# Projection weights of the second mixer, split into rounded part and remainder by casting and adding transfers instead of by ScalarE and VectorE

## The chip, the cores and the metric

The kernel runs on one core of a Trainium2 chip. Its time is the device time of one execution in microseconds, taken as the median of several runs. TensorE does the matrix products, VectorE and ScalarE the elementwise work, GpSimd (POOL in the profile) a few small operations and the issue of some transfers, SyncE (SP) the issue of most transfers. Sixteen DMA engines move the bytes.

## The reference, cut to what matters

The program is two layers of a hybrid backbone over 512 latent tokens and 256 context tokens of width 1024. The change concerns the mixer of the second layer, a bidirectional gated recurrence with 8 heads of width 128. For every head three column blocks of one input projection are needed, each a 1024 x 128 slice of the weights:

```python
h = jnp.concatenate([h_ctx, h_lat], axis=1)
fq, f_fwd, f_bwd, fi, fog = _split(h @ w_in, ODD_SIZES)      # w_in: (1024, 5 * 1024)
q = _heads(jax.nn.silu(fq), HGRN_HEADS)
for d, f in enumerate((f_fwd, f_bwd)):
    log_f = jnp.logaddexp(jnp.log(lb[d]), jnp.log1p(-lb[d]) + jax.nn.log_sigmoid(_heads(f, HGRN_HEADS)))
    k = -jnp.expm1(log_f)
    dirs.append(_directional_scan(q, k, i, log_f, n_ctx, reverse=(d == 1)))
o_lat = _gated_readout(dirs[0][1] + dirs[1][1], og[:, :, n_ctx:], out_norm)
```

All values are 32-bit floats.

## The kernel before, in words

**Three products for one.** A product of two 32-bit matrices is made of three products in the faster `float32r` type: each operand is split into a rounded part H and a remainder L = x - H, and H·H + H·L + L·H is accumulated (`mm3`, `gemm_T`). The activations are split beforehand. The weights are split as they arrive, in `fetched`/`unit` (L793 to L806): SyncE loads a unit of 1024 floats per partition into a `raw` tile (L799), ScalarE writes H by a casting copy (L803), VectorE writes L by a subtraction (L804). H and L lie in tiles with the tags `wH` and `wL`, four buffers each, `raw` has three.

**The stage.** `odd_mixer` runs over the 8 heads. `prep(hd)` makes, for direction 0, then direction 1, then the query, one product of a weight unit with the activations: `ff` twice (768 tokens, in a group of 256 and one of 512) and `fq` once (512 tokens). So the heads use 24 units in the order forward gate, backward gate, query. Between them stands the work of the recurrence of earlier heads: ScalarE copies and VectorE multiplications in turn (`qkh`, L1012; `arr`, L1017), small products (`pch`, `pbh`, `knph`, `pdh`, `kcT`, `poh`, `S`), and `rs`, a power on GpSimd (L686), whose result VectorE needs at once (L1489). Generators are advanced in a written-out order:

```python
for hd in range(8):
    given = []
    new = prep(hd, given)
    go(scan, new)
    go(outs, old)
    go(new, new)
    go(outs, old, scan)
    go(new, new)
    go(scan, scan)
```

**What sets the order.** Inside this loop `self.pinned` is true: every TensorE instruction keeps its place in program order (`pin`). ScalarE, VectorE and GpSimd work that isn't pinned is put in order by the framework's scheduler, which simulates the program with its own costs and issues what is ready; what is pinned stays behind all that the program has issued before it on that engine. On the chip each engine then runs its list strictly in that order, waiting where an operand isn't there yet. A tile gets a buffer of its tag when an earlier tile of that tag is done with.

After the heads, `gate` takes the units of the output gate through `wide_units`, by the same `unit`. The feed-forward block's down projection, earlier in the program, already contains transfers that add to what lies in SBUF: 36 of them, issued by GpSimd with `accum_op=ALU.add` (L1773), in pieces of 2 KB. The units of the second mixer are read from the weights in pieces of 128 floats, 512 bytes.

Of the kernel before, what the change touches and what calls it, by code (L numbers as in the profile page):

```python
# [316 lines left out]
class Net:  # L317
# [472 lines left out]
    def unit(self, src, k, n, pool=None, to=None):  # L790

        return self.fetched(src, k, n)(pool, to)
# [607 lines left out]
    def odd_mixer(self, h, fi):  # L1400
        nc, I = self.nc, self.I
        w = I["odd_w_in"][0]
        with self.pool("hg") as gp:
            ones = gp.tile([P, CTX], F32, tag="ones", name="ones")
            nc.gpsimd.memset(ones, 1.0)
            def prep(hd, given):

                f = gp.tile([P, 2, SEQ], F32, tag="f", bufs=2, name=f"f{hd}")
                arr = gp.tile([P, 4, SEQ], F32, tag="arr", bufs=2, name=f"arr{hd}")
                ks = gp.tile([P, SEQ], F32, tag="ks", bufs=2, name=f"ks{hd}")  # L1410
                S0, kcs = [], []
                for d in range(2):
                    pt = self.mm_tile(f"ff{hd}{d}")
                    W = self.unit_cols(w, (1 + d) * D + hd * P)
                    self.gemm_T(pt, W, h, ((512, 256),))
                    yield
                    self.gemm_T(pt, W, h, ((0, 512),))
                    sg = gp.tile([P, NT], F32, tag="sg", bufs=2, name="sg")
                    nc.scalar.activation(sg, pt[:, :NT], AF.Sigmoid)
                    lb, lb1, nlb1 = (x[:, d, hd : hd + 1] for x in (self.lb, self.lb1, self.nlb1))  # L1420
                    fc = gp.tile([P, CTX + 32], F32, tag="fc", bufs=2, name="fc")
                    kc = gp.tile([P, CTX], F32, tag="kc", bufs=2, name="kc")
                    nc.vector.tensor_scalar(fc[:, :CTX], sg[:, SEQ:], lb1, lb, op0=ALU.mult, op1=ALU.add)
                    nc.scalar.activation(kc, sg[:, SEQ:], AF.Identity, bias=lb1, scale=nlb1)
                    nc.vector.tensor_scalar(f[:, d, :], sg[:, :SEQ], lb1, lb, op0=ALU.mult, op1=ALU.add)
                    nc.scalar.activation(arr[:, 2 * d, :], sg[:, :SEQ], AF.Identity, bias=lb1, scale=nlb1)

                    pr = gp.tile([P, CTX], F32, tag="pr", bufs=1, name="pr")
                    if d == 0:
                        nc.vector.memset(pr[:, CTX - 1 : CTX], 1.0)  # L1430
                        nc.vector.tensor_tensor_scan(
                            pr[:, 0 : CTX - 1][:, ::-1], fc[:, 1:CTX][:, ::-1], ones[:, 1:CTX], 1.0, op0=ALU.mult, op1=ALU.mult
                        )
                    else:
                        nc.vector.memset(pr[:, 0:1], 1.0)
                        nc.vector.tensor_tensor_scan(
                            pr[:, 1:CTX], fc[:, 0 : CTX - 1], ones[:, 1:CTX], 1.0, op0=ALU.mult, op1=ALU.mult
                        )
                    nc.vector.tensor_tensor(kc, kc, pr, op=ALU.mult)

                    kcs.append(kc)
                    yield
                pq = self.mm_tile(f"fq{hd}")
                self.gemm_T(pq, self.unit_cols(w, hd * P), h, ((0, 512),))
                q = gp.tile([P, SEQ], F32, tag="q", bufs=2, name=f"q{hd}")
                nc.scalar.activation(q, pq[:, :SEQ], AF.Sigmoid)
                nc.vector.tensor_tensor(q, q, pq[:, :SEQ], op=ALU.mult)
                nc.vector.tensor_tensor(arr[:, 1, :], q, f[:, 1, :], op=ALU.mult)
                nc.vector.tensor_tensor(arr[:, 3, :], q, f[:, 0, :], op=ALU.mult)
                nc.vector.tensor_tensor(ks, arr[:, 0, :], arr[:, 2, :], op=ALU.add)  # L1450
                given.append((arr, q, ks, f, S0))
                yield
                kns = []
                for kc in kcs:
                    pk = self.tr_tile("kcT")
                    for i in range(2):
                        self.tr(pk[:, i * P : (i + 1) * P], kc[:, i * P : (i + 1) * P], self.ident)
                    kn = gp.tile([P, CTX], F32, tag="kcn", bufs=2, name="kcn")
                    nc.scalar.copy(kn, pk[:, :CTX])
                    kns.append(kn)  # L1460
                yield
                pS = self.sc_tile("S0")
                for d, kn in enumerate(kns):
                    for i in range(2):
                        self.mm(
                            pS[:, d * P : (d + 1) * P],
                            kn[:, i * P : (i + 1) * P],
                            fi[:, LT + i, hd * P : (hd + 1) * P],
                            start=(i == 0),
                            stop=(i == 1),  # L1470
                        )
                for d in range(2):
                    S = gp.tile([P, P], F32, tag="S0", bufs=4, name=f"S0{hd}{d}")
                    nc.scalar.copy(S, pS[:, d * P : (d + 1) * P])
                    S0.append(S)

            def head(hd, arr, q, ks, f, S0):
                def V(t, hh):
                    return fi[:, t, hd * P : (hd + 1) * P]

                def evac(hh, t0, n, po):
                    o = fi[:, 0:LT, hd * P : (hd + 1) * P]
                    nc.scalar.copy(o, po)
                    sq = gp.tile([P, LT, P], F32, tag="sq", bufs=1, name="sq")
                    nc.scalar.activation(sq, po, AF.Square)
                    ss = self.sm.tile([P, LT], F32, tag="ss4", name="ss4")
                    nc.vector.tensor_reduce(ss, sq, axis=AX.X, op=ALU.add)
                    rs = self.rstd(ss, P, LT)
                    nc.vector.tensor_tensor(o, o, rs[:, :, None].to_broadcast([P, LT, P]), op=ALU.mult)  # L1489

                return self.scan(gp, f"h{hd}", arr, q, ks, 1.0, f, LT, 1, V, S0, None, evac)

            def gate(c0, early):
                us = self.wide_units(4 * D + c0)
                for t0 in (0, 2):
                    s = self.wp.tile([P, WU], F32, tag="mraw", bufs=2, name="silu").rearrange("p (a n) -> p a n", a=2)

                    def apply(x, t0=t0, s=s):
                        o = fi[:, t0 + x.start : t0 + x.stop, c0 : c0 + 512]
                        nc.vector.tensor_tensor(o, o, s[:, x, :], op=ALU.mult)  # L1500

                    for a in range(2):
                        pt = self.mm_tile("nat")[:, :512]
                        self.wide_tile(pt, us, h, t0 + a)
                        nc.scalar.activation(s[:, a, :], pt, AF.Silu)
                        if t0 or not early:
                            apply(slice(a, a + 1))
                        yield
                    if early and t0 == 0:
                        apply(slice(0, 2))  # L1510

            def go(*xs):
                for x in xs:
                    next(x, None)

            self.pinned = True
            outs = old = scan = iter(())
# [9 lines that stand above are left out]
                outs, old, scan = scan, new, head(hd, *given[0])  # L1527
            g = [gate(0, False), gate(512, True)]
            go(scan, g[0])
            go(outs, old)  # L1530
            go(g[0])
            go(outs, old, scan)
            go(g[0], g[0])
            go(scan, scan)
            go(g[1])
            go(scan)
            go(g[1])
            go(scan)
            go(g[1], g[1])
            self.pinned = False  # L1540

        cat = Split(h.pool)
        for _ in self.gated_T(lambda t, hh: fi[:, t, hh * P : (hh + 1) * P], 8, R_HG, cat, ((0, 4),)):
            pass
        return cat
# [739 lines left out]
```

## Time and profile before

| | |
|---|---|
| median of 3 runs | 1674.94 us (1674.29 to 1675.55) |
| the profiled execution | 1675.78 us, its span 1674.0 us |
| busy over the span | PE 1644.8, DVE 1311.1, ACT 916.1, POOL 129.4 us |
| granted TensorE clock | 0.998 |
| the 24 units of the heads | used from 982 to 1219 us |
| one head, 1094.97 to 1126.50 us | 31.53 us: PE 31.53, DVE 25.13, ACT 19.69, POOL 1.43 busy |

PE is TensorE's matmuls, PEld its weight loads, DVE is VectorE, ACT ScalarE, POOL GpSimd. In a row of groups stand the line, the engine, the operation, output<-inputs, the number of instructions, the busy time, the mean of one in ns, and the idle time just before them with what ended it. All transfers issued by GpSimd run in the queue q0, those of SyncE in q1.

### The profile page before, as it was taken

Reading aid. Unit: us, or ns where it says so; the run is one execution under the profiler, and the core shown is the slowest. Engines: PE = TensorE matmul, PEld = TensorE weight load, DVE = VectorE, ACT = ScalarE, POOL = GpSimd, SP = SyncE. Lnnn points to the kernel's source line nnn. Section 1 sums busy time; section 2 is a strip of 40 time slices with the busy share of each in tenths; the row PEclk is TensorE's granted clock in tenths of the full one; section 3 lists DMA queues with packets and bytes.
Section 4 is the critical chain, followed back from the end, with each engine's and each line's share of the span. In section 5 each row is a group of like instructions: output and inputs, shape, how many; then the busy total and the mean of one; then the engine's idle time right before and its main releaser. Section 6 shows DMA issues by size and latency. Waiting matters only on the chain.

```text
span 1674.0 us, 32524 instructions
## 1 busy us (share of the span) xinstructions
PE 1644.8 (98%) x13407; PEld 1481.1 (88%) x13407; DVE 1311.1 (78%) x2097; ACT 916.1 (55%) x1551; POOL 129.4 (8%) x139
## 2 busy tenths in 40 slices
PE   9999999999999999999999999999999999999998
PEld 7899987888999999998887888888888899999886
DVE  5999678976898988777668648788775599987887
ACT  5745567845544443446447436666664565555664
POOL 2004110011000000002102000000000100000310
PEclk9999999999999999999999999999999999999999
DMA  9641012164243445249525541121124333333973
GB/s 336 213 132 41 3 45 86 50 227 160 80 126 114 139 151 176 78 153 205 100 84 193 200 127 57 48 65 40 51 65 150 126 114 115 114 101 102 226 164 138
DMA packets 184736, 204.79 MB, mean 122 GB/s; under 512 B 7142, under 2 KB 141836, under 8 KB 184588
## 3 DMA queue, kind: packets, MB, share of 16 engines
q1 hardware_dynamic: 173996, 181.98, 34.7%
q0 software_dynamic: 9024, 17.30, 5.9%
q10 hardware_dynamic: 1568, 3.43, 0.6%
q8 instruction: 105, 1.72, 0.4%
q14 instruction: 43, 0.35, 0.1%
HBM read 193.23 MB, written 9.46 MB: 121 GB/s over the span
## 4 chain that ended last, share of the span: by engine, by line
PE 83%; DVE 8%; ACT 3%; DMA 3%; issue 2%; POOL 0%; SPq 0%; DVEq 0%; ACTq 0%; POOLq 0%
PE nat L355 12%; PE a L355 10%; PE ff L355 8%; PE E L355 7%; PE oproj L355 6%; PE x L355 6%; PE o L355 5%; PE D L355 4%; PE b L355 3%; PE fq L355 3%; PE gqk L355 2%; PE pearly L355 2%; PE q L355 2%; PE S L355 2%; PE poh L355 1%
## 5 line engine op out<-in xcount | busy, mean ns | idle before, releaser
L355 PE MATMUL nat<-wH,x 128*128 128x256 f32 (+2 forms) x968 | 226.7, 322 | 1.2 <-ACT x L2014 0.6
L860 ACT CAST wH<-raw 128x1024 fp32r<-128x1024 f32 x120 | 124.8, 1051 | 102.7 <-DVE raw L885 40.7
L355 PEld LDWEIGHTS nat<-wH,x 128*128 128x128 f32 x968 | 161.9, 190 | 19.5 <-ACT natq L1196 1.7
L861 DVE TENSOR_TENSOR wL<-raw,wH 128x1024 fp32r<-128x1024 f32 x120 | 145.7, 1222 | 23.6 <-ACT wH L860 23.3
L355 PE MATMUL nat<-wL,x 128*128 128x256 f32 (+2 forms) x484 | 153.5, 317 | 1.8 <-DVE wL L804 1.8
L804 DVE TENSOR_TENSOR wL<-raw,wH 128x1024 fp32r<-128x1024 f32 x79 | 95.8, 1222 | 50.6 <-ACT wH L803 49.8
L355 PE MATMUL ff<-x,wH 128*128 128x512 f32 (+1 forms) x512 | 127.6, 340 | 0.0
L686 POOL TENSOR_TENSOR rs<-ms,neghalf 128x1 f32<-128x1 f32 (+2 forms) x56 | 60.1, 1076 | 777.7 <-DVE ms L684 777.6
L803 ACT CAST wH<-raw 128x1024 fp32r<-128x1024 f32 x79 | 82.2, 1050 | 68.5 <-PE ff L355 19.7
L355 PE MATMUL oproj<-wH,x 128*128 128x512 f32 x320 | 102.2, 394 | 0.4 <-ACT x L1330 0.4
L355 PEld LDWEIGHTS nat<-wL,x 128*128 128x128 f32 x484 | 92.1, 190 | 7.8 <-DVE wL L804 2.7
L615 DVE SCALAR_TENSOR_TENSOR macc<-mraw,scT,macc 128x1024 f32<-128x1024 f32 x70 | 88.0, 1282 | 11.6 <-DMA mraw<-in_mod_w_dram 11.4
L355 PEld LDWEIGHTS ff<-x,wH 128*128 128x128 f32 x512 | 87.3, 190 | 10.0
L355 PE MATMUL x<-wH,two 128*128 128x512 f32 x280 | 90.5, 392 | 0.9 <-DVE y L1851 0.7
L1773 POOL DMA_DIRECT2D t<-in_ffn_w_down_dram x36 | 41.9, 1200 | 640.1 <-DVE t L1812 338.3
L1012 ACT COPY qkh<-arr 128x512 f32<-128x512 f32 x112 | 70.2, 641 | 36.6 <-DVE arr L1017 32.3
L355 PE MATMUL ff<-x,wL 128*128 128x256 f32 (+1 forms) x256 | 86.2, 337 | 0.0
L885 DVE TENSOR_TENSOR raw<-raw 128x512 f32<-128x512 f32 x120 | 82.8, 690 | 2.8
L1017 DVE TENSOR_TENSOR arr<-arr,f 128x512 f32<-128x512 f32 x112 | 74.4, 688 | 2.0 <-ACT qkh L1012 0.3
L355 PEld LDWEIGHTS oproj<-wH,x 128*128 128x128 f32 x320 | 59.9, 188 | 13.0 <-ACT x L1330 1.0
L355 PE MATMUL a<-T,wH 128*128 128x384 f32 (+1 forms) x320 | 70.5, 309 | 0.6 <-ACT qb L923 0.5
L355 PE MATMUL E<-T,wH 128*128 128x384 f32 (+1 forms) x320 | 70.4, 309 | 0.7 <-DVE go L938 0.7
(425 smaller groups left out, 4558.6 us busy)
## 6 DMA issues: line engine op xcount, KB each, us to landing
mraw<-in_mod_w_dram SPq DMA_DIRECT2D x80, 512.0 KB, 4.4
raw<-in_ffn_w_gate_dram SPq DMA_DIRECT2D x44, 512.0 KB, 3.9
raw<-in_ffn_w_up_dram SPq DMA_DIRECT2D x44, 512.0 KB, 4.9
raw<-in_odd_w_in_dram SPq DMA_DIRECT2D x40, 512.0 KB, 3.7
t<-in_ffn_w_down_dram POOLq DMA_DIRECT2D x30, 512.0 KB, 8.3
raw<-in_ffn_w_down_dram SPq DMA_DIRECT2D x28, 512.0 KB, 8.0
mraw<-in_mod_w_dram SPq DMA_DIRECT2D x32, 256.0 KB, 6.3
raw<-in_even_w_in_dram SPq DMA_DIRECT2D x16, 512.0 KB, 5.9
```

The lines of the kernel that those rows point to most:

```text
L355: return self.pin(self.nc.tensor.matmul(*a, **k))
L615: nc.vector.scalar_tensor_tensor(a, u, w, a, op0=ALU.mult, op1=ALU.add)
L686: nc.gpsimd.tensor_tensor(rs, ms, self.neghalf.to_broadcast([P, w]), op=ALU.pow)
L803: self.casts = self.casts[-1:] + [nc.scalar.copy(H[:, :m], raw[:, :m])]
L804: vector.tensor_tensor(L[:, :m], raw[:, :m], H[:, :m].bitcast(F32), op=ALU.subtract)
L860: self.nc.scalar.copy(H, f)
L861: self.nc.vector.tensor_tensor(L, f, H.bitcast(F32), op=ALU.subtract)
L885: add = lambda o, x, y: nc.vector.tensor_tensor(o, x, y, op=ALU.add)
L1012: nc.scalar.copy(qkv[:, :, :, half, :], dst)
L1017: nc.vector.tensor_tensor(dst, dst, tb, op=ALU.mult)
L1773: add = lambda o, src: self.pin(nc.gpsimd.dma_start(out=o, in_=src, accum_op=ALU.add))
```

## The change

The heads' units are numbered 0 to 23. Units 0 to 2 are fetched as before. For unit n from 3 on, a call of `unit` three units ahead allocates H and L and lets GpSimd issue two casting transfers of 256 KB each from the weights into H (`rounded`). Two units ahead of its use ScalarE writes -H into L, and GpSimd issues two transfers of 256 KB that add the weights to L (`remainder`), so that L = w - H. The `raw` tile, SyncE's load, the casting copy and the subtraction are gone for these 21 units; the four new transfers of each are pinned.

```diff
+            units = {}
+
+            def rows(n):
+                c0 = (D, 2 * D, 0)[n % 3] + n // 3 * P
+                return w[:, c0 : c0 + P].rearrange("(k p) m -> p k m", p=P)
+
+            def rounded(n):
+                H, L = [self.wp.tile([P, WU], F32R, tag=f"w{x}", bufs=4, name=f"w{x}") for x in "HL"]
+                units[n] = [x.rearrange("p (k m) -> p k m", k=KD) for x in (H, L)]
+                for k in (slice(0, 4), slice(4, 8)):
+                    self.pin(nc.gpsimd.dma_start(out=units[n][0][:, k, :], in_=rows(n)[:, k, :]))
+
+            def remainder(n):
+                H, L = units[n]
+                nc.scalar.mul(L, H.bitcast(F32), -1.0)
+                for k in (slice(0, 4), slice(4, 8)):
+                    self.pin(nc.gpsimd.dma_start(out=L[:, k, :], in_=rows(n)[:, k, :], accum_op=ALU.add))
+
+            def unit(n):
+                if n + 3 < 24:
+                    rounded(n + 3)
+                if 3 <= n + 2 < 24:
+                    remainder(n + 2)
+                return units.pop(n) if n in units else self.unit(rows(n), KD, P)
+
...
-                    W = self.unit_cols(w, (1 + d) * D + hd * P)
+                    W = unit(3 * hd + d)
...
-                self.gemm_T(pq, self.unit_cols(w, hd * P), h, ((0, 512),))
+                self.gemm_T(pq, unit(3 * hd + 2), h, ((0, 512),))
```

## The prediction

> **What bounds the kernel now.** I read the page's first part, then the table by stretches for one head, the waits from 980 to 1240 us (the stage of the change), and the chain that ended last through that head.
>
> ```profile
> span 1674.0 us, 32524 instructions
> PE 1644.8 (98%) x13407; PEld 1481.1 (88%) x13407; DVE 1311.1 (78%) x2097; ACT 916.1 (55%) x1551; POOL 129.4 (8%) x139
> 1094.97:1126.50 31.53, 31.53 (x400) 28.10 (x400) 25.13 (x57) 19.69 (x35) 1.43 (x1) 1.00 0.18 52
> PEld pch L355 <- issue: 2.5, 7, 0.4
> PE gcT L358 <- DVE gc L662: 1.0, 1, 1.0
> 1099.62 8.35 PE ff L355 x48
> 1118.48 5.44 PE fq L355 x24
> 1126.50 2.88 PE ff L355 x24
> 1129.37 1.34 PE pdh L355 x12
> ```
>
> The third row is one head: PE is busy 31.53 of 31.53 us at clock 1.00, DVE 25.13, ACT 19.69, POOL 1.43, the DMA engines 18% of the time. The waits list many pairs, but only two in which TensorE stands (total, times, longest): 1.0 us once, at the start of the stage, for VectorE's `gc`, and 0.4 us a head in its own sequencer. The last four rows are the chain (start, duration): products one behind the other. They hide no wait: the 24 large matmuls inside the 8.35 us of `ff` take 8.35 - 2.88 = 5.47 us, the 24 equal ones of `fq` 5.44. TensorE sets the pace of the stage, and VectorE and ScalarE wait for it or for each other.
>
> **The change, part by part.**
>
> *What goes from VectorE and ScalarE.*
>
> ```profile
> L804 DVE TENSOR_TENSOR wL<-raw,wH 128x1024 fp32r<-128x1024 f32 x27 | 33.0, 1224 | 29.8 <-ACT wH L803 29.6
> L803 ACT CAST wH<-raw 128x1024 fp32r<-128x1024 f32 x26 | 27.3, 1049 | 36.0 <-PE ff L355 19.7 <-PE fq L355 16.1 <-PE nat L355 0.3
> ```
>
> VectorE loses 21 subtractions of 1.224 us, 25.7 us in all or 3.7 a head. ScalarE loses 21 casts and gets 21 negations of the same shape, which I take at the same 1.05 us: nothing. All of this ran beside TensorE, so on the path it saves 0. At most the 1.0 us wait for `gc` shrinks, behind fewer subtractions; I take 0. SyncE loses 21 loads; nobody waited for them in the stage.
>
> *What is added on GpSimd and the DMA queues.* 84 transfers of 256 KB in 512-byte pieces, 12 a head. The nearest rows are the adding transfers of the down projection, in 2 KB pieces, in a stretch (800 to 825 us) where little else moves, and SyncE's present loads of the same weights (1000 to 1200 us):
>
> ```profile
> 802.68 0.91 POOL L1773 DMA_DIRECT2D t<-in_ffn_w_down_dram  x1 [23.77 <-DVE wL L1807]
> 806.94 1.22 POOL L1773 DMA_DIRECT2D t<-in_ffn_w_down_dram  x1 [3.35 <-DVE wL L1807]
> q0 software_dynamic: 1301, 2.50, 65.2%
> q1 hardware_dynamic: 267, 0.51, 6.8%
> t<-in_ffn_w_down_dram POOLq DMA_DIRECT2D x5, 512.0 KB, 5.8
> t<-in_ffn_w_down_dram POOLq DMA_DIRECT2D x1, 256.0 KB, 4.2
> ...
> q1 hardware_dynamic: 17728, 10.49, 18.2%
> 1113.48 1.43 POOL L686 TENSOR_TENSOR rs<-ms,neghalf 128x4 f32<-128x4 f32 x1 [30.09 <-DVE ms L684]
> ```
>
> Issue: 128 pieces (256 KB) cost GpSimd 0.91 us, 256 pieces 1.22. A new transfer has 512; another 256 at 0.31 per 128 make 1.84. Bounds: 0.91 (pieces don't count) and 3.6 (proportional). I take 1.84, along the line through the two rows: 12 x 1.84 + 1.43 = 23.5 of 31.5 us. GpSimd stays under the period.
>
> Bytes: a 2 KB piece that adds took 0.652 x 25 x 16 / 1301 = 0.20 us of an engine, a plain one of about 2 KB 0.068 x 25 x 16 / 267 = 0.102, a plain one of about 0.5 KB 0.182 x 200 x 16 / 17728 = 0.033. Plain cost goes nearly with the bytes (a third at 0.6 KB), so I take a third of 0.20, 0.065 us, for an adding 512-byte piece; bounds 0.033 and 0.20. For a casting one, which no row shows, the same bounds, and 0.033 to 0.065. Each engine gets 32 pieces of a transfer: a head's 192 + 192 pieces take 192 x (0.065 + 0.033 to 0.065) = 19 to 25 us of 31.5. They fit too.
>
> Landing: 256 KB landed in 4.2 = 0.91 + 8 x 0.20 + 1.7, 512 KB in 5.8 = 1.22 + 16 x 0.20 + 1.4. So a transfer lands 1.5 us after its issue, plus its pieces.
>
> *Where the new waits stand.* On GpSimd the first casting transfer of unit n+3 waits for TensorE's last matmul with unit n-1, whose buffer it takes. Behind it are queued its second half, the two adding transfers of unit n+2 (which wait for ScalarE's negation), and the next `rs`. Tightest is the second `ff` unit of a head: `ff` ends at 1118.48; casting transfers issue to 1122.2, adding ones to 1125.8, and the last adding pieces land at about 1130. TensorE wants them at 1105.09 + 31.53 = 1136.6 (1105.09 is where that `ff` began, 1099.62 + 5.47). 6 us are left. `rs` at 1113.48 comes after four issues that start at 1105.1 and end at 1112.5: free.
>
> On ScalarE a negation waits for the landed H, and what is listed behind it waits as well:
>
> ```profile
> 1118.73 1.05 ACT L803 CAST wH<-raw 128x1024 fp32r<-128x1024 f32 x1
> 1121.03 0.80 ACT L1426 ACTIVATE arr<-sg,lb,nlb 128x512 f32<-128x512 f32 x1
> 1124.68 0.59 ACT L1446 ACTIVATE q<-fq 128x512 f32<-128x512 f32 x1
> 1126.22 0.87 ACT L1064 COPY knh<-knph 128x384 f32<-128x384 f32 x2
> ACT wH L803 <- DMA raw<-in_odd_w_in_dram: 3.3, 2, 2.0
> ```
>
> The scheduler orders ScalarE by its own idea of when H lands; the last row (whole run) shows it early by up to 2.0 us. After 1121.8 ScalarE is free until `fq` ends, so the negation for the unit cast from 1118.48 on may be listed ahead of `q`. H's second half lands at 1118.48 + 2 x 1.84 + 1.5 + 32 x 0.033 = 1124.7, with 0.065 us a piece (the first half in the way) at 1126. Then negation, `q`, and 2.41 us from the start of `q` to the end of `knh`. `pdh` needs `knh` at 1129.37: `q` may start at 1126.96, H may land at 1125.9. So it just holds; I take 0, and every microsecond later costs 1 us in each of six heads (the units 8, 11, ... 23). The other two negations of a head have more room: what they hold back is next needed 5 us later or more.
>
> *The start.*
>
> ```profile
> 949.38 1.05 ACT L803 CAST wH<-raw 128x1024 fp32r<-128x1024 f32 x1 [2.01 <-DMA raw<-in_odd_w_in_dram]
> 981.13 1.05 ACT L803 CAST wH<-raw 128x1024 fp32r<-128x1024 f32 x1
> 998.78 1.05 ACT L803 CAST wH<-raw 128x1024 fp32r<-128x1024 f32 x1 [3.78 <-PE ff L355]
> 999.87 1.23 DVE L804 TENSOR_TENSOR wL<-raw,wH 128x1024 fp32r<-128x1024 f32 x1 [4.05 <-ACT wH L803]
> 999.26 0.39 PE L355 MATMUL fq<-x,wL 128*128 128x512 f32 x1
> ```
>
> Before, units 0 to 3 are cast by 981.13 into the four buffers. Now units 3, 4 and 5 are asked for before 0, 1 and 2 respectively, so six units share four buffers, and unit 2, the first query, can end up with the buffer that unit 1 frees at 998.8. Its cast and subtraction then take the place that unit 5's had in the rows: L is there at 999.87 + 1.23 = 1001.10, and the first matmul with L, at 999.26 before, waits 1.8 us. Ends: 0 if unit 2 gets an earlier buffer, 3 if the first adding transfers come late too. I take 1.8, as six units can't lie in four buffers.
>
> *Sum.* Against the profiled execution, 1675.78 us: 0 + 0 + 1.8 = 1677.6. That execution is 0.84 above the median of the three runs, so 1676.8 stands against 1674.94. That is 0.11%; 0.2%, or 3.35 us, is about what a measurement of this kernel can tell from no change.
>
> [...]
>
> **The rivals.**
>
> *ScalarE is held by a landing (slower).* The place is the negation ahead of `q`; it decides from H landing over 7.4 us after `ff` ends. For it: the issue queue of GpSimd stands ahead of the landing, the 2.0 us row, and 7.9 us was the median landing in the busier down projection. Against: VectorE is 3.7 us a head less loaded, and the cast at 1118.73 no longer stands ahead. At 1 to 3 us late: 6 to 18 us, 1683 to 1695, mid 1687.
>
> ```profile
> DMA to landing us min/median/max: 4.2/7.9/12.2
> ```
>
> *The DMA engines become the bound (slower).* If a piece costs 0.20 us whatever its size, when it adds: a head takes 192 x (0.20 + 0.033) = 44.7 us against 31.5, over seven heads 92 us: 1767. Cast pieces at 0.20 as well make 76.8 a head and 1992. It decides from 0.131 us an adding piece. Against: plain pieces get cheaper with size.
>
> *GpSimd becomes the bound (slower).* It decides from 2.5 us an issue (12 x 2.5 + 1.43 = 31.4). At 3.0, 37.4 us a head, 41 us in seven: 1716. Against: the two measured issues lie on a flat line.
>
> *VectorE's relief is worth something (faster).* Its 25.13 of 31.53 us fall to 21.4, and if the 1.0 us and all seven sequencer waits of 0.4 went, 3.5 us: 1671.4. Against: no other wait of TensorE is there to remove.
>
> **How the numbers follow.** Forecast (start only, 1676.8): 0.50. ScalarE held: 0.29, of which 0.03 stay within 0.2%. DMA bound 0.10. GpSimd bound 0.06. Faster 0.05. So slower by over 0.2%: 0.26 + 0.10 + 0.06 = 0.42; within: 0.53; faster: 0.05. The forecast's own range is 1674 to 1678.3. To leave out no more than 2 in 10 it must reach over the held ScalarE: up to 1700, with the two bounds (0.16) and a gain of over 1 us (0.03) outside.
>
> **What would show it.** Right: the period of a head stays 31.5 us with PE full; a DVE of about 21.4 a head; GpSimd's issues near 1.8 us; no wait of PE for ScalarE or DMA after 1010 us; a wait of up to 2 us before the first `fq`. Wrong: PE waiting for `knh` in every head with ScalarE's `wL` waiting for a transfer (first rival), for `wL` itself with q0 busy all the time (second) or with GpSimd busy all the time (third). The weakest step is the price of a 512-byte casting or adding piece, which no row shows.

## The result, and the profile after

The changed kernel takes 1702.43 us (median of 3 runs, 1699.45 to 1705.98) against 1674.94: 1.0165 of the time before, interval 1.0133 to 1.0197. The profiled execution is the slowest of the three, 1705.98 us with a span of 1704.2, so its numbers run some 3.5 us above the median. The forecast was 1676.8 with a range up to 1700: the time lies 25.6 us above the one and 2.4 us outside the other.

The first part and the transfers of the page of after:

```profile
span 1704.2 us, 32616 instructions
PE 1657.3 (97%) x13407; PEld 1490.7 (87%) x13407; DVE 1289.6 (76%) x2076; ACT 913.4 (54%) x1551; POOL 215.1 (13%) x223
wH<-in_odd_w_in_dram POOLq DMA_DIRECT2D x42, 256.0 KB, 3.7
wL<-in_odd_w_in_dram POOLq DMA_DIRECT2D x42, 256.0 KB, 4.7
```

The same number of products now keeps PE busy 12.5 us longer, and the span grows by 30.2. VectorE loses 21.5 us, GpSimd gains 85.7. The table by stretches (length, then PE, PEld, DVE, ACT, POOL busy, clock, DMA share, GB/s), for two heads in the middle of the stage and for the last one, in which only two casting and four adding transfers are left to issue:

```profile
1062.00:1100.30 38.30, 34.22 (x398) 30.39 (x397) 22.07 (x54) 19.25 (x34) 13.68 (x13) 0.91 0.56 84
1100.30:1137.80 37.50, 34.10 (x398) 30.27 (x397) 22.69 (x55) 19.51 (x35) 13.60 (x13) 0.91 0.58 86
1211.90:1243.50 31.60, 31.60 (x400) 28.17 (x399) 26.02 (x62) 21.20 (x37) 8.15 (x7) 1.00 0.47 85
```

A head went from 31.53 to some 38 us. Some 3.4 to 4.1 us of that is PE standing still, and some 2.6 is PE busy for longer, at a mean clock of 0.91. No engine but PE is near full and the DMA engines are little over half busy, so the columns alone name no bound. The waits of the stage (970 to 1290 us; total, times, longest) do:

```profile
POOL wL L1422 <- issue: 83.2, 31, 5.6
ACT wL L1420 <- DMA wH<-in_odd_w_in_dram: 73.1, 16, 9.3
DVE arr L1017 <- ACT qkh L1012: 42.8, 6, 8.9
POOL wH L1416 <- issue: 42.6, 17, 3.9
PE poh L355 <- DVE Sh L1084: 9.7, 5, 2.2
PE poh L355 <- ACT kcn L1484: 4.9, 4, 1.9
PE pdh L355 <- DVE CTh L997: 2.7, 1, 2.7
PE fq L355 <- ACT wH L803: 0.9, 1, 0.9
PE fq L355 <- DVE wL L804: 0.5, 1, 0.5
```

Read from the bottom: TensorE stands 17.3 us in three new waits inside the heads and 1.4 us at the first `fq`. With the 12.5 us of longer busy time that is 31.2, against 30.2 of growth. The first row is the surprise. "Issue" is time in which the engine waited for nothing that the profile shows: GpSimd stood 126 us, 18 a head, ahead of transfers whose operands were there. Its timeline (start, duration, idle before):

```profile
1019.74 1.31 POOL L1422 DMA_DIRECT2D wL<-in_odd_w_in_dram  x1
1024.60 1.30 POOL L1422 DMA_DIRECT2D wL<-in_odd_w_in_dram  x1 [3.55 <-issue]
1025.45 1.23 POOL L1416 DMA_DIRECT2D wH<-in_odd_w_in_dram  x1
1029.67 0.76 POOL L1416 DMA_DIRECT2D wH<-in_odd_w_in_dram  x1 [2.99 <-issue]
```

An issue is cheap, some 0.8 us for a casting transfer and 1.3 for an adding one; but in the four transfers of a unit GpSimd stops twice for about 3 to 4 us, about until something earlier has landed: the add issued at 1019.74 landed 4.5 us later, and the next one starts at 1024.60. The waits on GpSimd in the two heads from 1062 to 1137.8 us:

```profile
POOL wL L1422 <- issue: 26.2, 9, 5.5
POOL wH L1416 <- issue: 12.5, 4, 3.9
POOL wH L1416 <- PE ff L355: 5.0, 2, 2.9
POOL wL L1422 <- ACT kc L1449: 2.1, 1, 2.1
POOL wL L1422 <- ACT arr L1451: 2.1, 1, 2.1
```

Issuing and `rs` 13.68 + 13.60 = 27.3 us, stops 38.7: 33.0 us a head, more than the 31.53 that TensorE needs. The two waits of 2.1 us, put down to ScalarE, look like stops too: each ends 0.3 us after the landing of the first of the two casting transfers ahead of it (issued at 1063.12 and 1101.91, landed 3.4 us later). With them it is 35.1 us a head. The last 5.0 us, for the buffer of `ff`, are the way back: GpSimd waits for a TensorE that is late. The chain shows how GpSimd's load reaches TensorE (start, duration):

```profile
1111.90 0.77 POOL wH L1416
1112.67 3.94 issue
...
1116.62 3.38 DMA wH<-in_odd_w_in_dram
...
1120.07 1.06 ACT wL L1420
1121.13 0.56 ACT qkh L1012
...
1121.71 1.29 DVE arr L1017 x2
...
1127.56 3.35 PE poh L355 x14
```

The second half of an H is issued 3.94 us late, lands at 1120.0, and holds ScalarE's negation; `qkh` is listed behind the negation, VectorE's `arr` (L1017) waits for `qkh`, `Sh` for `arr`, and `poh` for `Sh`. TensorE, late, frees the next buffer late, and the next casting transfer starts late again.

### The profile page after: what moved, and what is told of

The parts are those of the page before. It is cut to its first block, busy times and chain, and to the rows that moved or that the text cites. A ratio compares the mean times of both kernels' runs of the same rounds, so it can differ in the third digit from the quotient of the medians.

```text
span 1704.2 us, 32616 instructions
## 1 busy us (share of the span) xinstructions
PE 1657.3 (97%) x13407; PEld 1490.7 (87%) x13407; DVE 1289.6 (76%) x2076; ACT 913.4 (54%) x1551; POOL 215.1 (13%) x223
## 4 chain that ended last, share of the span: by engine, by line
PE 72%; DVE 10%; issue 7%; ACT 4%; DMA 3%; POOL 3%; DVEq 0%; SPq 0%; POOLq 0%; ACTq 0%
PE nat L355 12%; PE a L355 10%; PE E L355 7%; PE x L355 7%; PE oproj L355 6%; PE o L355 5%; PE b L355 3%; PE D L355 3%; PE ff L355 3%; PE gqk L355 2%; PE pearly L355 2%; POOL wL L1422 2%; PE q L355 2%; PE S L355 1%; PE attO L355 1%
## 5 line engine op out<-in xcount | busy, mean ns | idle before, releaser
L860 ACT CAST wH<-raw 128x1024 fp32r<-128x1024 f32 x120 | 124.8, 1051 | 100.7 <-DVE raw L885 38.7
L861 DVE TENSOR_TENSOR wL<-raw,wH 128x1024 fp32r<-128x1024 f32 x120 | 145.8, 1222 | 24.0 <-ACT wH L860 23.4
L686 POOL TENSOR_TENSOR rs<-ms,neghalf 128x1 f32<-128x1 f32 (+2 forms) x56 | 59.2, 1062 | 561.2 <-DVE ms L684 561.0
L1017 DVE TENSOR_TENSOR arr<-arr,f 128x512 f32<-128x512 f32 x112 | 73.9, 689 | 44.5 <-ACT qkh L1012 42.8
L804 DVE TENSOR_TENSOR wL<-raw,wH 128x1024 fp32r<-128x1024 f32 x58 | 70.1, 1222 | 34.0 <-ACT wH L803 33.2
L1012 ACT COPY qkh<-arr 128x512 f32<-128x512 f32 x112 | 69.0, 637 | 30.2 <-DVE arr L1017 26.1
L803 ACT CAST wH<-raw 128x1024 fp32r<-128x1024 f32 x58 | 60.1, 1050 | 39.1 <-PE nat L355 17.0
L355 PE MATMUL E<-x,wH 128*128 128x384 f32 (+1 forms) x320 | 70.6, 310 | 0.0
```

The lines of the kernel that those rows point to most:

```text
L355: return self.pin(self.nc.tensor.matmul(*a, **k))
L686: nc.gpsimd.tensor_tensor(rs, ms, self.neghalf.to_broadcast([P, w]), op=ALU.pow)
L803: self.casts = self.casts[-1:] + [nc.scalar.copy(H[:, :m], raw[:, :m])]
L804: vector.tensor_tensor(L[:, :m], raw[:, :m], H[:, :m].bitcast(F32), op=ALU.subtract)
L860: self.nc.scalar.copy(H, f)
L861: self.nc.vector.tensor_tensor(L, f, H.bitcast(F32), op=ALU.subtract)
```

## The experiments

**Taking GpSimd's stops away, and using each kind of transfer alone.** Theory A: the pieces under way at once are limited, an adding piece counts as two, and GpSimd stops until there is room. Rival B: an adding transfer waits for the one before it, whatever its size. Rival C: the DMA engines are the bound. The first kernel below tells the three apart; the other two, where A and B forecast the same, show what each kind of transfer costs by itself.

With the adds in four quarters:

```diff
-                for k in (slice(0, 4), slice(4, 8)):
+                for k in (slice(0, 2), slice(2, 4), slice(4, 6), slice(6, 8)):
                     self.pin(nc.gpsimd.dma_start(out=L[:, k, :], in_=rows(n)[:, k, :], accum_op=ALU.add))
```

> Edit: each unit's remainder is added by four transfers of 128 KB instead of two of 256 KB. Theory A (room for pieces in flight: GpSimd stops issuing when more than 1536 to 2047 pieces of 512 bytes would be under way, an adding piece counting twice): three of the smaller adding transfers fit at once, so the stops of 3.7 and 2.9 us in each unit shrink to under 1 us each, GpSimd's cycle falls from 11 to about 7 us a unit, and the time comes back to 1676 to 1685 us. Theory B (after an adding transfer GpSimd lets only one further transfer go until it has landed, whatever its size): four stops of 2.5 to 3 us a unit, over 14 us a unit, 42 us or more a head, and the time goes above 1740 us. Theory C (the DMA engines are the bound): the bytes are the same, so the time stays near 1702.

1677.50 us, 1.0017 of before (1.0007 to 1.0026). The same bytes in the same pieces, in more transfers, and nearly all of the 27 us is gone. Its table for two heads and its waits from 970 to 1290 us:

```profile
1062.00:1093.50 31.50, 31.50 (x417) 28.07 (x404) 22.04 (x53) 18.10 (x34) 20.09 (x19) 1.00 0.71 102
1093.50:1125.00 31.50, 31.12 (x358) 27.61 (x344) 22.13 (x53) 19.77 (x35) 20.82 (x20) 1.00 0.69 102
```

```profile
ACT wL L1420 <- DMA wH<-in_odd_w_in_dram: 54.4, 19, 4.7
POOL wL L1422 <- issue: 28.2, 30, 2.7
POOL wH L1416 <- issue: 4.9, 8, 1.0
PE fq L355 <- ACT wH L803: 0.9, 1, 0.9
PE fq L355 <- DVE wL L804: 0.5, 1, 0.5
```

GpSimd issues for longer (20.5 us a head with `rs`) but stops for 33.1 / 7 = 4.7 us instead of 18. Together 25.2 of 31.5. ScalarE still waits for landings, 2.9 us at a time in the mean instead of 4.6, and that costs TensorE next to nothing in the heads (0.4 us at `poh`). B, with twice as many adds to wait for, and C, with the same pieces, both fall. The DMA engines, busy 71% here against 56, show the same.

H by casting transfers, L by SyncE's load and VectorE's subtraction as before:

```diff
-                nc.scalar.mul(L, H.bitcast(F32), -1.0)
-                for k in (slice(0, 4), slice(4, 8)):
-                    self.pin(nc.gpsimd.dma_start(out=L[:, k, :], in_=rows(n)[:, k, :], accum_op=ALU.add))
+                raw = self.wp.tile([P, WU], F32, tag="raw", bufs=3, name="raw")
+                nc.sync.dma_start(out=raw.rearrange("p (k m) -> p k m", k=KD), in_=rows(n))
+                nc.vector.tensor_tensor(L, raw.rearrange("p (k m) -> p k m", k=KD), H.bitcast(F32), op=ALU.subtract)
```

> Edit: the rounded part is still written by two casting transfers, but the remainder comes from SyncE's load and VectorE's subtraction as before the change; ScalarE has no part. Theory A: two casts a unit leave room, no stops on GpSimd, 1675 to 1682 us. Theory B: the same. Theory C: a piece that only casts is cheap, the same. If instead the waiting for a landed cast alone is what costs, VectorE is held in the place of ScalarE and the time stays above 1690 us.

1677.91 us, 1.0024 (1.0014 to 1.0033). Stops of GpSimd in the stage: 0.8 us in all. VectorE now waits 16.4 us for casts to land, 2.8 at most, and in the heads TensorE doesn't notice: such waits for a landed cast cost nothing by themselves in this run.

H by ScalarE from SyncE's load, L by negation and adding transfers:

```diff
-                for k in (slice(0, 4), slice(4, 8)):
-                    self.pin(nc.gpsimd.dma_start(out=units[n][0][:, k, :], in_=rows(n)[:, k, :]))
+                raw = self.wp.tile([P, WU], F32, tag="raw", bufs=3, name="raw")
+                nc.sync.dma_start(out=raw.rearrange("p (k m) -> p k m", k=KD), in_=rows(n))
+                nc.scalar.copy(units[n][0], raw.rearrange("p (k m) -> p k m", k=KD))
```

> Edit: the rounded part is cast by ScalarE from SyncE's load as before the change; only the remainder is made by ScalarE's negation and the two adding transfers. Theory A: one stop of about 3.5 us a unit is left, between the two adding transfers; GpSimd uses 6 to 7 of 10.5 us a unit and nothing waits for a cast to land, 1675 to 1682 us. Theory B: the same. Theory C (engine time of adding pieces): if they were the bound, the time would stay near 1702 us.

1677.13 us, 1.0018 (1.0009 to 1.0028). The row of waits on GpSimd shows that the stops alone are not the price:

```profile
POOL wL L1423 <- issue: 101.0, 27, 6.2
```

101 us of stops, 14 a head, and TensorE doesn't notice, since half of the transfers are gone and GpSimd's list still fits into the head (9.3 us of issues and `rs`, 14.4 of stops). It takes both kinds together to fill it.

**Taking the landing off ScalarE's path.** If a negation that waits for its landing ahead of `qkh` is the cause, holding it to the order of the program should mend it; if GpSimd is the bound, it shouldn't.

```diff
-                nc.scalar.mul(L, H.bitcast(F32), -1.0)
+                self.tc.keep_in_program_order(nc.scalar.mul(L, H.bitcast(F32), -1.0))
```

> Edit: ScalarE's negation is pinned to its place in program order, behind all ScalarE work issued before it, so that it no longer stands early in ScalarE's list waiting for a cast to land; GpSimd's list is the same. If ScalarE held by late casts is what reaches TensorE: the 8 us holds of ScalarE go, 1676 to 1685 us although GpSimd still stops. If GpSimd's own cycle (33 to 34 us of issues and stops a head) is the floor: 1690 us or more, and TensorE waits for the weights themselves.

1721.29 us, 1.0283 (1.0268 to 1.0298): worse. Waits, 970 to 1290 us:

```profile
POOL wL L1422 <- issue: 79.8, 28, 5.1
DVE fi L1514 <- POOL rs L686: 53.1, 7, 11.4
POOL wH L1416 <- issue: 52.5, 21, 4.3
POOL wL L1422 <- ACT wL L1420: 41.2, 8, 11.9
PE pbh L355 <- ACT qkh L1012: 23.5, 5, 5.9
```

GpSimd's stops are 132 us, much as the 126 of after. Now its adds wait for the later negation on top, `rs` stands behind the adds, VectorE's `fi` waits for `rs` up to 11.4 us, and TensorE stands at `pbh` instead of `poh`. The first expectation falls: ScalarE no longer waits for a landing, and the time is worse. Of the second the time holds, but TensorE waits only 0.6 us for the weights themselves. How much of it is still GpSimd's stops, the next kernel shows. With both edits, the pinned negation and the adds in quarters:

```diff
+                self.tc.keep_in_program_order(nc.scalar.mul(L, H.bitcast(F32), -1.0))
+                for k in (slice(0, 2), slice(2, 4), slice(4, 6), slice(6, 8)):
```

> Both edits at once: the negation held to the order of the program on ScalarE, and the adding transfers as four of 128 KB. If GpSimd's stops were the root of the pinned kernel's 1721.3 us too: the waits of ff's halo on ScalarE's qkh and of fi on rs shrink to a few us, and the time falls to 1676 to 1682. If the pinned order by itself was the cause (the negation comes too late for the adds, whatever their size): the time stays above 1700, with rs behind the adds as before.

1690.86 us, 1.0096 (1.0082 to 1.0110), between the two: with the stops down to 19.4 us, 30 of the 47 us by which the pinned kernel stood above before are gone. The table by stretches splits the rest:

```profile
980.00:1020.00 40.00, 31.56 (x161) 26.78 (x160) 10.84 (x24) 12.60 (x18) 13.95 (x14) 0.91 0.61 111
1020.00:1220.00 200.00, 197.05 (x2431) 174.92 (x2430) 139.28 (x329) 121.08 (x214) 124.16 (x115) 1.00 0.66 96
```

In the heads from 1020 us on TensorE loses 3 us in 200: with few stops the pinned order nearly fits. In the first 40 us it stands 8.4 us, at a clock of 0.91, waiting for VectorE's `pr` (3.8) and `wL` (3.1). The span grew by 14.8 us; these two take 7.5 (against 39.03 busy of those 40 us before) and 3, and some 4 us show only as longer busy time. So the pinned order has a price of its own, at the start, and neither expectation foresaw that.

**The limit by itself.** The kernel before, with bursts of seven transfers on the idle GpSimd into a tile that nobody reads, after heads 2 to 6. The first burst (i = 0) is of casts of 512 pieces of 512 bytes, the second of adds of the same, the third of adds of 256 such pieces, the fourth of adds of 128 pieces of 2 KB, the fifth of casts of the same:

```diff
+            def burst(i):
+                for j in range(7):
...
+                    self.pin(nc.gpsimd.dma_start(out=to, in_=src, **({"accum_op": ALU.add} if i in (1, 2, 3) else {})))
```

> The kernel before, with work added that serves nothing: at the ends of heads 2 to 6 the idle GpSimd issues a burst of seven transfers back to back into a scratch tile. First burst: casting, 512 pieces of 512 bytes each. Second: adding, 512 pieces of 512 bytes. Third: adding, 256 pieces of 512 bytes. Fourth: adding, 128 pieces of 2 KB. Fifth: casting, 128 pieces of 2 KB. Theory A (the pieces that are under way at once are limited, an adding piece counts twice, the limit lies between 1536 and 2047): first burst, three transfers about 0.8 us apart, then one per landing, each stopped; second burst, the second transfer already stops for about 3.4 us, and so each after it; third burst, three go, then stops of about 1 to 1.5 us; fourth burst, at least six go without a stop; fifth, no stop. Theory B (an adding transfer waits until the adding one before it has landed, whatever its size): the second, third and fourth bursts stop at every transfer for some 2 to 3.5 us, the first and the fifth never. Theory C (the stops come only where TensorE, ScalarE and DMA queues contend with it): stops scattered with no regard to the size. Time: within 3 us of the kernel before, as GpSimd's work lies beside TensorE's.

One run, 1674.97 us; the kernel before on the same chip 1674.72. The timeline of GpSimd, bursts in order (rows of `rs` left out):

```profile
1050.68 2.34 POOL L1419 DMA_DIRECT2D probe<-in_odd_w_in_dram  x3
1054.59 0.75 POOL L1419 DMA_DIRECT2D probe<-in_odd_w_in_dram  x1 [1.56 <-issue]
...
1082.24 1.32 POOL L1419 DMA_DIRECT2D probe<-in_odd_w_in_dram  x1
1087.30 1.31 POOL L1419 DMA_DIRECT2D probe<-in_odd_w_in_dram  x1 [3.74 <-issue]
...
1116.00 1.79 POOL L1419 DMA_DIRECT2D probe<-in_odd_w_in_dram  x1
1119.22 5.06 POOL L1419 DMA_DIRECT2D probe<-in_odd_w_in_dram  x4 [1.43 <-issue]
...
1146.12 6.37 POOL L1419 DMA_DIRECT2D probe<-in_odd_w_in_dram  x7
...
1177.66 3.80 POOL L1419 DMA_DIRECT2D probe<-in_odd_w_in_dram  x7
```

Casts of 512 pieces: three go, the fourth stops. Adds of 512: every one after the first stops, 3.6 to 5.2 us. Adds of 256: the first goes beside the last large add; the second waits 1.43 us, until that add has landed; then it and three more go nearly in a row, and the sixth and seventh stop for 0.15 and 0.74 us. Adds and casts of 128 pieces of 2 KB: all seven go. The second and the fourth burst move the same bytes in transfers of the same size and the same kind; only the number of pieces differs. So in these bursts neither the bytes nor the order of adds (B) makes GpSimd stop; its stops go with the pieces under way, and they follow the shape of the burst, not the other work around it (C, as it stands in this expectation). Three casts of 512 fit and four don't, one add of 512 fits and two don't: that agrees with an add counted twice and room for 1536 to 2047, an estimate from these stops. The third burst narrows it. Its fifth, sixth and seventh transfers (at 1123.1, 1124.4 and 1126.4 us) each start 0.2 to 0.3 us after the landing of the one three before (issued at 1119.2, 1120.0 and 1121.0, landed after 3.6, 4.2 and 5.1 us). So three adds of 256 are under way at once and a fourth is not: 768 adding pieces fit and 1024 don't, where 1536 casting pieces do. By this estimate an adding piece takes the room of 1.5 to 2.7 casting ones. The expected sizes of these stops, 1 to 1.5 us, were too large, as the landings came while GpSimd still issued. The bursts of 128 pieces agree, since seven of them are 1792 even counted twice. The time, like that of before, says again that stops, here 29.5 us in all, cost nothing where nobody waits for GpSimd.

**The 3 us that are left.** With quartered adds the first `fq` still waits 0.9 + 0.5 us, as unit 2 finds its buffer taken. The kernels with one kind of transfer have the same wait, and some 3 us too. Three kernels, all with quartered adds, try to remove that wait. Units 3 to 5 asked for only behind unit 2:

```diff
+                W = units.pop(n) if n in units else self.unit(rows(n), KD, P)
+                for m in (3, 4, 5) if n == 2 else (n + 3,):
+                    if n >= 2 and m < 24:
+                        rounded(m)
...
```

> The adding transfers as four of 128 KB, and units 3, 4 and 5 asked for only behind units 0, 1 and 2, so that unit 2 no longer waits for a buffer that a later unit took. If the 3 us that the kernel with four adding transfers keeps over the kernel before are the late first fq (waits of 0.9 and 0.5 us) and what follows from it: both waits are gone from the view of waits, and the time is 1674.5 to 1676. If they come from a cost in every head (contention of 84 casting and 84 adding transfers with the others): 1677 to 1678 with the fq waits gone. Faster than the kernel before by over 0.2% by neither, since TensorE is busy all the time.

1681.06 us, 1.0037 (1.0023 to 1.0050). The wait at `fq` is gone, but three units now come at once: `ff` waits 1.0 us for the adding transfers and `pdh` 1.2 for `CTh`. Between 980 and 1050 us PE is busy 66.56 us, against 68.02 with quartered adds alone and 69.03 before.

The first two heads as in the kernel before:

```diff
-                if n + 3 < 24:
+                if 6 <= n + 3 < 24:
...
-                if 3 <= n + 2 < 24:
+                if 6 <= n + 2 < 24:
```

> The adding transfers as four of 128 KB, and the first six units (heads 0 and 1) made as in the kernel before, by SyncE, ScalarE and VectorE; only units 6 to 23 by casting and adding transfers. If the 3 us that are left with four adding transfers in all heads come from the start, where unit 2 waits for a buffer: the waits of fq on wH and wL (0.9 and 0.5 us) are gone and the time is 1674.3 to 1675.7, within 0.1% of the kernel before. If they come from every head (more traffic beside TensorE): three quarters of them stay, 1676.5 to 1677.5, with TensorE's waits inside the heads as before. Faster than the kernel before by over 0.2% by neither.

1677.41 us against 1675.44 on that chip, 1.0014 (1.0005 to 1.0023). The wait at `fq`, again 0.9 + 0.5 us, only moved to the next head (1023.81 us): unit 5 now finds its buffer taken. The time lies in the range of the second expectation, but no wait of TensorE in every head stands behind it.

The lead grown step by step (unit 3 asked for behind unit 1, 4 behind 2, 5 behind 3, 6 and 7 behind 4):

```diff
+                asked = ((), (3,), (4,), (5,), (6, 7))
+                for m in asked[n] if n < 5 else (n + 3,):
+                    if m < 24:
+                        rounded(m)
...
```

> The adding transfers as four of 128 KB, and the lead of the new units grown step by step, so that no unit of the old kind finds its buffer taken: unit 3 is asked for behind unit 1, unit 4 behind unit 2, unit 5 behind unit 3, units 6 and 7 behind unit 4, and from there three ahead as before. If the late unit at the change from the old kind to the new is what the kernel with four adding transfers still pays: no wait of fq on wH or wL, no wait on a landing in heads 0 and 1, and 1674.5 to 1676. If a shorter lead makes these units late (a lead of two units is 21 us, the way of a unit over casting, negation and adding some 16 to 20): a wait of ff on a landing of 1 to 4 us in head 1, 1677 to 1681. If each head pays: 1677 to 1678 with no such wait. Faster than the kernel before by over 0.2% by none.

1681.39 us, 1.0040 (1.0027 to 1.0054). No wait at `fq`; with the shorter lead ScalarE waits up to 8.9 us for a landing and `poh` 2.5 us for `Sh` and 1.5 us for `kcn`. None came down to the kernel before; the last came nearest to its second expectation, a lead too short, though not by the wait of `ff` named there. Wherever the change from the old kind of unit to the new was put, it cost TensorE waits of 1.4 us or more. Whether all of the last 3 us are that stays open; the profiled execution with quartered adds was only 1.24 us above the profiled one of before (1677.02 against 1675.78). No version beat the kernel before.

## Why the prediction was wrong, point by point

- **What bounds the kernel.** Right. PE was full, VectorE's relief came (a head 25.13 us to 22.1, 21.4 forecast) and bought nothing: with quartered adds PE runs 31.50 and 31.12 of 31.5 us in two heads, and the time is not below before.
- **GpSimd's price, the step that failed.** "GpSimd stays under the period", at 12 x 1.84 + 1.43 = 23.5 us. The issue itself was cheaper than taken: 6 x 0.78 + 6 x 1.31 = 12.5 us a head. But the step knew no other cost of a transfer on GpSimd than its issue, and let every issue start as the one before ended. The stops for room add 18 us a head. In the two heads above 24.2 us of issue and 38.7 of stops make 62.9 / 24 = 2.62 us a transfer, past the 2.5 us from which the third rival decides. That rival, "GpSimd becomes the bound", had a chance of 0.06 because "the two measured issues lie on a flat line": true of the issue, and beside the point. Both rows stood alone, 23.77 and 3.35 us after the engine's last work, with 128 and 256 pieces; no row quoted was of transfers as large in pieces, or as close together, as those of the change.
- **The held negation.** The first rival's mechanism appears, but at another place. The prediction put it at the negation ahead of `q` and said of the others that they "have more room: what they hold back is next needed 5 us later or more". It was one of these, the first unit's ahead of `qkh`, that reached `poh`: in the units 9, 12, ... 21 it waited 7.2 to 9.3 us, past that room of 5, where the mean of all negations that waited is 4.6. It is a consequence: with the stops shortened the mean fell to 2.9 us, the longest to 4.7, and nothing was lost. (That rival's 1683 and 1695 are counted from 1676.8, its 1687 and the other rivals' times from 1674.94; nothing rests on the 1.9 us between.)
- **Pieces.** Right in size. From 1010 to 1200 us:

```profile
q0 software_dynamic: 32819, 16.30, 58.6%
```

  0.586 x 190 x 16 / 32819 = 0.054 us a piece, casting and adding together. The kernels with one kind each give, over the same stretch, 0.262 x 190 x 16 / 18537 = 0.043 for a casting piece and 0.414 x 190 x 16 / 19324 = 0.065 for an adding one; 0.033 to 0.065 and 0.065 were taken. The DMA engines bound nothing, as forecast; the second rival falls.
- **The start.** 1.8 us forecast, 1.4 measured, at the buffer and the unit named. It is as large as the whole difference between the profiled executions of the quartered kernel and of before, 1.24 us; by the medians the difference is 3 us, and the rest is open.
- **The landing.** 3.7 us casting and 4.7 adding. From the formula, issue + 1.5 + pieces, with the measured issues: 0.78 + 1.5 + 32 x 0.033 = 3.3 and 1.31 + 1.5 + 32 x 0.065 = 4.9. Right.

## What to carry over

Before moving transfers to GpSimd, count the pieces under way, not only issues and bytes: an engine that stands at "issue" ahead of transfers with their operands ready may be waiting for room, as GpSimd was here by the estimate from the bursts (126 us of stops in the stage), and what is listed behind stands too. Where an adding transfer in small pieces can't be avoided, try smaller transfers: here four of 128 KB in the place of two of 256 KB took the stops from 18 to 4.7 us a head. Price an issue from rows as dense as the new list will be, and check the sum of issue and stops against the period.

## What the runs showed of the hardware that was not expected

**Room for pieces.** In the bursts on the idle GpSimd three casting transfers of 512 pieces of 512 bytes went and the fourth stopped for 1.56 us; every adding transfer of 512 pieces after the first stopped, for 3.64 to 5.19 us; of adding transfers of 256 pieces three were under way at once and a fourth wasn't. An estimate from these stops and landings: GpSimd stops when its next transfer would bring the pieces under way past a number between 1536 and 2047 for casting pieces of 512 bytes, and between 768 and 1023 for adding ones. It went on 0.2 to 0.4 us after a whole transfer had landed, in the bursts as in after. An adding piece counted as two is the simplest reading; the bursts allow 1.5 to 2.7. What it is that fills up, no run shows.

**The clock after a pause.** In a stalled head of after, in the table by stretches:

```profile
1082.00:1086.00 4.00, 2.11 (x18) 1.91 (x17) 2.39 (x6) 3.83 (x7) 1.13 (x2) 1.00 0.49 61
1086.00:1090.00 4.00, 1.81 (x12) 1.62 (x13) 4.00 (x12) 2.63 (x5) 1.19 (x3) 0.81 0.87 131
1090.00:1094.00 4.00, 4.00 (x21) 4.00 (x20) 1.39 (x4) 0.74 (x1) 1.91 (x2) 0.50 0.42 73
1094.00:1098.00 4.00, 4.00 (x140) 3.40 (x140) 1.50 (x3) 3.94 (x10) 1.36 (x2) 0.83 0.50 64
```

TensorE stands 4.1 of the 8 us from 1082 to 1090, and from about 1 us before the end of its second wait, at 1089.45, the granted clock is 0.50: the last three rows lack (0.19 + 0.50 + 0.17) x 4 = 3.4 us of clock, so 6.9 us at half. PE is busy 34.22 us in that head and 31.60 in the last one, so behind two waits of 1.89 and 2.19 us it is busy 2.6 us longer. The stage has four such stretches, and their missing clock, a little of it while TensorE stood, adds up to 12.0 us (0.17 x 20 in 1030 to 1050, 1080 to 1100 and 1120 to 1140 us, 0.09 x 20 in 1190 to 1210); before has a clock of 1.00 in all of them. PE's longer busy time, 12.5 us or 40% of the loss, is read as this, the author's estimate; no run held the clock, so it isn't tested, and no step of the prediction had it. With more DMA traffic, 102 GB/s against 84 to 86, and waits of 0.4 us at most inside the heads (quartered adds) the clock is 1.00 in the two heads shown. No wait of TensorE in this stage is longer than 2.7 us. One of 2.71 us (ending at 1038.08 us), or two of 1.1 to 1.9 and 2.19 us, went with a stretch at half clock; two of 0.69 and 2.19 us (ending at 1161.37 and 1164.94 us) went with none, at 1.00 from 1160 to 1180 us. How long a wait it takes, these rows don't show.
